# A one-core DiT block: mLSTM products with tokens on partitions, gathered tokens turned once, a smaller first modulation group, and the last dense batch cut in two

## The chip, the cores and the metric

The kernel runs on one core of one Trainium2 chip. The metric is device microseconds of one execution. Times are medians of several runs; the rows below come from one profiled execution of the kernel before.

## The reference

One layer of a diffusion backbone on 256 latent tokens and 256 context tokens of width 2048, in float32. The context is only read by the mLSTM. Cut to what matters here:

```
m_lat, m_ctx = silu(c) @ ada_w + ada_b, silu(c_ctx) @ ada_w + ada_b     # six modulation vectors each
hc = modulate(rmsnorm(x_ctx, norm_mix), m_ctx[0], m_ctx[1])
hl = modulate(rmsnorm(x_lat, norm_mix), m_lat[0], m_lat[1])
pl = hl @ w_in                                                # all heads; hc @ w_in[:, OFF_K:] for the context

# mLSTM, 4 heads x 2 directions, chunks of 128 tokens, one step of the scan:
s   = einsum('bhtd,bhsd->bhts', qc, kc) * exp(log_w - m_t)
num = einsum('bhts,bhsv->bhtv', s, vc) + w_prev * einsum('bhvk,bhtk->bhtv', C, qc)
den = s.sum(-1) + w_prev * einsum('bhk,bhtk->bht', n, qc)
h   = num / maximum(abs(den), exp(-m_t))
# then h_f + h_b, hn = h * rsqrt(mean(h * h, -1) + EPS), sigmoid(o) * hn * g

x_lat = x_lat + m_lat[2] * (y_l @ w_out)                      # y_l: sgu, mLSTM and pooling side by side
hf = modulate(rmsnorm(x_lat, norm_ffn), m_lat[3], m_lat[4])
# PEER: hf @ wq, scores with 2 x 128 keys, top 16 of the 16 x 16 sums: 128 experts per token;
# a = hf . u_tab[e]; w = softmax(scores) * gelu(a); out = sum of w * v_tab[e]
return rmsnorm(x_lat + m_lat[5] * peer_ffn(hf, ...), norm_final)
```

## The kernel before

**Layout and engines.** Activations lie with channels on partitions (xL latent, xC context, 16 tiles of 128 channels by 256 tokens). Weights come in units of 512 KB from HBM on SP's queue (`load`, L273). A unit is copied on ACT to a rounded `hi` part, the rest is formed on DVE as `lo`, and TensorE (PE) multiplies in three passes (hi by hi, hi by lo, lo by hi): 24 matmuls of 256 columns for a unit, tiles named `mm`. One helper records each matmul (L354) and one each DVE and ACT operation (L133), so the tile names tell rows apart. A float32 matmul shows as two records of PE in the trace, one in the listings of the order.

**Order.** All instructions are emitted in one stream per engine by a planner: each stage is a generator that emits a piece and yields an estimated time, and the planner runs beside each other the units of the projections (`step`), the heads (`gen_heads`), the second modulation (`araw`, `adacc`, `adat`), and later the copying of tokens (`copy_hB`). PE has PSUM banks of three tags: `mm` (4 banks), `sm` (3) and one for `ada`.

**The start.** `ada` weights (2 of the 6 modulation vectors) come in 32 ring loads of 1 MB, 5 in flight (RING). Four groups of 512 channels of 8 ring loads each: PE multiplies (`adaps`), ACT copies (`adasb`), PE turns the result onto partitions (`adat`), and DVE forms four operations per 128 channels (`hm`, `xL`, `hm`, `xC`). The first units `wf` (gates and a part of K) are accumulated over the 16 channel tiles, so each of their pieces waits for its group.

**The heads.** For each head and direction `weights` forms sT (source tokens by tokens) and qw; `products` makes num^T (channels on partitions, 128 x 512) by 8 matmuls and den by 7 matmuls of one column; `diagonal` puts 1/den on a diagonal (2 ACT operations) and `spread_out` multiplies it by ones, so that each row holds it (tile `all`). `finish` scales num, and `norm` squares, sums over channels by 8 records of one column (`hss`), again goes through `diagonal` and `spread_out`, and scales.

**PEER.** 64 of the 256 tokens gather their u rows, through one copy of the tokens in rows (`hB`, four tokens' copies of each, half of them at a time); 192 tokens are multiplied densely with the whole u table (`ups`). Then the v rows are gathered: 1 MB per token for the 192 dense tokens, 32 tokens in a batch accumulated in one `y`; `finish(b, y)` turns a batch back, adds the residual, makes the last rmsnorm and stores 256 KB.

Of the kernel before, what the change touches and what calls it, by code (L numbers as in the profile page):

```python
# [32 lines left out]
P = 128  # L33
D = 2048
# [42 lines left out]
LAG = 3.0  # L77
SUB = 8
# [13 lines left out]
AFTER = 1  # L92
PREP = 1
SS_AT = 2
EARLY = 1
LOAD_AT = {2: 1, 3: 1, 4: 1}
FIRST_AT = (3,)
# [81 lines left out]
def build(tc, a, stack, dbg=None):  # L179
# [219 lines left out]

    early = con.tile([P, 1152], F32, name="early", tag="st")  # L400
# [4 lines left out]
    def ada_mm(ps, kp, w):  # L405
        for kk in range(2):
            for part in range(2):
                j = 2 * kk + part
                mm(ps[32 * j:32 * j + 32, :], st[:, 2 * kp + kk, :], w[:, kk, part * 512:part * 512 + 512],
                   start=(kp == 0), stop=(kp == KD // 2 - 1), tile_position=(0, 32 * j))  # L410

    def ada_fin(g, ps, work, tag):

        sb = work.tile([P, 512], F32, name="adasb", tag=tag, bufs=4)
        act.activation(sb, ps, AF.Copy)
        yield 2.0
        pt = sm_ps("adat")
        for q in range(4):
            mm(pt[:, 4 * q:4 * q + 4], sb[:, q * P:(q + 1) * P], sel.rearrange("p a i -> p (a i)"),
               start=True, stop=True)  # L420
        ptv = pt[:, 0:16].rearrange("p (q a i) -> p a i q", a=2, i=2)
        k4 = slice(4 * g, 4 * g + 4)
        for part in range(2):
            b = vecs[:, V_ADAB + part * KD + 4 * g:V_ADAB + part * KD + 4 * g + 4]
            vec.tensor_tensor(mod[:, part, :, k4], ptv[:, part], b[:, None, :].to_broadcast([P, 2, 4]), op=OP.add)
        for i in range(2):
            vec.scalar_tensor_tensor(gm[:, i, k4], mod[:, 1, i, k4], 1.0,
                                     vecs[:, V_NMIX + 4 * g:V_NMIX + 4 * g + 4], op0=OP.add, op1=OP.mult)
        yield 0.0
# [92 lines left out]
    def add_first(src, streams, dones, n_ada, rest):  # L522


        box = {}

        def use(n, q):
            def f(u):
                if q == 0:
# [3 lines left out]
                for kt in range(4):  # L533
# [11 lines left out]

        for q in range(4):
            for n in range(3):
                add(src[n, q], True, use(n, q))
                if q == 3:
                    add_ada(n_ada)  # L550
                    rest(n)
# [31 lines left out]
    def alloc_mixers():  # L583
# [11 lines left out]
        V["Ct"] = b1[:, 4096:8192].rearrange("p (r k v) -> p r k v", r=8, k=2)  # L595
        V["ncol"] = early[:, 1000:1016].rearrange("p (r k) -> p r k", k=2)
        V["kT"] = B.tile([P, 8, T], F32, name="kT")
        V["vlat"] = B.tile([P, 2, 1024], F32, name="vlat")
# [120 lines left out]
    def vm_done(cb):  # L719
        def f(pss):  # L720
            s = slice(cb * 512, cb * 512 + 512)
            for i in range(2):
                act.activation(V["vctx"][:, i, s], pss[2 + i], AF.Copy)
                act.activation(V["vlat"][:, i, s], pss[i], AF.Copy)
# [6 lines left out]
    def gen_C(h, d):  # L731
# [8 lines left out]
        for kt in range(2):  # L740
# [4 lines left out]
            act.activation(V["Ct"][:, r, kt], pc[:, 0:T], AF.Copy)  # L745
            vec.tensor_copy(V["ncol"][:, r, kt:kt + 1], pc[:, T:T + 1])
# [21 lines left out]
    def gen_heads():  # L768
        B, kT, qT, vlat, Ct = V["B"], V["kT"], V["qT"], V["vlat"], V["Ct"]
        rows3, gtok, mask, ncol = V["rows3"], V["gtok"], V["mask"], V["ncol"]  # L770
# [38 lines left out]
        def products(h, d, sT, rng, qw):  # L809
            r, row = d * 4 + h, d * 32 + h  # L810

            blks = (0, 1) if d == 0 else (1, 0)
            pn = mm_ps("num")
            for vt in range(2):
                o = pn[:, vt * T:(vt + 1) * T]
                for n, blk in enumerate(blks):
                    t0, t1 = rng[blk]
                    mm(o[:, t0:t1], vlat[:, blk, h * T + vt * P:h * T + (vt + 1) * P], sT[:, blk, t0:t1],
                       start=(vt == 0 and n == 0), stop=False)
                for kt in range(2):  # L820
                    mm(o, Ct[:, r, kt, vt * P:(vt + 1) * P], qw[:, kt], start=False, stop=(vt == 1 and kt == 1))

            pd = sm_ps("den")
# [10 lines left out]
            return pn, diagonal(den)  # L834

        def diagonal(x):
            dg = B.tile([P, 2, P], F32, name="diag", tag="nB", bufs=1)
            for tb in range(2):
                act.activation(dg[:, tb], ident, AF.Copy, scale=x[:, tb:tb + 1])
            return dg  # L840

        def spread_out(dg):

            pb = sm_ps("all")
            for tb in range(2):
                mm(pb[:, tb * P:(tb + 1) * P], ones, dg[:, tb], start=(tb == 0), stop=(tb == 1))
            return pb[:, 0:T]

        def finish(h, d, pn, dg):
            den = B.tile([P, T], F32, name="E", tag="E", bufs=1)  # L850
            act.activation(den, spread_out(dg), AF.Copy)
            den_b = den[:, None, :].to_broadcast([P, 2, T])
            pnv = pn.rearrange("p (b t) -> p b t", b=2)
            if d == 0:
                hold["hs"] = B.tile([P, 2, T], F32, name="hs", tag="b1")
                vec.tensor_tensor(hold["hs"], pnv, den_b, op=OP.mult)
            else:
                hb = big()
                vec.tensor_tensor(hb, pnv, den_b, op=OP.mult)
                vec.tensor_tensor(hold["hs"], hold["hs"], hb, op=OP.add)  # L860

        def norm(h):
            hs = hold["hs"]
            h2 = B.tile([P, 2, T], F32, name="h2", tag="b2")
            act.activation(h2, hs, AF.Square)
            yield HY4
            pq = sm_ps("hss")
            for tb in range(2):
                for vt in range(2):
                    mm(pq[:, tb:tb + 1], h2[:, vt, tb * P:(tb + 1) * P], ones[:, 0:1],  # L870
                       start=(tb == 0 and vt == 0), stop=(tb == 1 and vt == 1))
            rs = B.tile([P, 2], F32, name="hrs", tag="den", bufs=2)
            rstd_of(rs, pq[:, 0:2], T)
            dg = diagonal(rs)
            yield HY5
            while V.get("o", -1) < 2 * h + 1:
                yield 1.0
            yb = V["yb"][:, 2 * h:2 * h + 2]
            vec.tensor_tensor(hs, hs, spread_out(dg)[:, None, :].to_broadcast([P, 2, T]), op=OP.mult)
            vec.tensor_tensor(yb, yb, hs, op=OP.mult)  # L880

        for h in range(HEADS):
            scores(h)
            yield 2.0
            for d in range(2):
                rest = weights(h, d)
                yield HY1
                pn, dg = products(h, d, *rest)
                yield HY2
                finish(h, d, pn, dg)  # L890
# [199 lines left out]
    hBd = tc.dram_tile([P, D], F32, name="hB_spill")  # L1090

    def copy_hB():

        hf, h64 = R["hf"], R["h64"]
        yield HBY0
        for k0 in range(0, KD, 4):
            k4 = slice(k0, k0 + 4)
            vec.tensor_tensor(h64[:, k4], hf[:, k4, 0, NA:T].bitcast(F32), hf[:, k4, 1, NA:T].bitcast(F32), op=OP.add)
            for g in range(2):
                yield HBY if g == 0 else 1.0  # L1100
                pbt = sm_ps("hbt")
                for k in range(k0, k0 + 4):
                    for r in range(REP):
                        mm(pbt[r * BT:(r + 1) * BT, (k - k0) * P:(k - k0 + 1) * P], h64[:, k, g * BT:(g + 1) * BT],
                           ident, start=True, stop=True, tile_position=(0, r * BT))
# [652 lines left out]
```

## Time and profile before

| what | us |
|---|---|
| median of 3 runs | 1932.53 (1932.23 to 1934.69) |
| profiled execution | 1929.97 |
| its span, first to last instruction | 1928.2 |
| PE busy | 1710.3 (89%) |
| weight loads of PE (beside PE) | 1354.9 (70%) |
| DVE busy | 1226.9 (64%) |
| ACT busy | 701.6 (36%) |
| POOL busy | 382.9 (20%) |

The profiled execution is 2.6 us under the median, and 1.8 us of it lie outside the span. The DMA engines move 670 MB in the span, 348 GB/s in the mean. Busy shares are means over stages with different limits: the table of stretches below tells which engine fills which stage.

### The profile page before, as it was taken

What the parts mean: (1) busy time and instruction counts of PE and PEld (TensorE: products, weight loads), DVE (VectorE), ACT (ScalarE), POOL (GpSimd) and SP (SyncE); (2) the same over time, 40 slices, a digit from 0 to 9 for tenths busy, and PEclk for the clock granted to TensorE, in tenths of its full rate; (3) what the DMA queues carried; (4) which work ended last, traced back from release to release, by engine and by line L of the source; (5) the groups of instructions that cost most, each with busy time, mean ns of one, the idle gap of its engine ahead of it and who ended that gap; (6) DMA issues with size and microseconds to landing.
All of it is one profiled execution on the core that took longest, in us unless ns stands there. A gap on an engine that the chain in (4) does not pass through costs nothing.

```text
span 1928.2 us, 29971 instructions
## 1 busy us (share of the span) xinstructions
PE 1710.3 (89%) x11882; PEld 1354.9 (70%) x11882; DVE 1226.9 (64%) x2498; ACT 701.6 (36%) x1105; POOL 382.9 (20%) x324
## 2 busy tenths in 40 slices
PE   4999999999899899899999899999997777767765
PEld 2689789979899799889888798888873222222221
DVE  5356868776698669989998787777553323323232
ACT  4235335555544444454444454444431101101010
POOL 0000000000000000432333233233223333333331
PEclk8999999999999999999999999999998888888898
DMA  9975878776778754999999999999989999999996
GB/s 395 392 268 186 286 243 294 272 251 221 230 290 329 261 182 151 370 420 417 417 409 419 396 421 421 415 397 392 383 325 409 421 421 421 421 421 421 420 421 276
DMA packets 115870, 670.20 MB, mean 348 GB/s; under 512 B 12689, under 2 KB 15249, under 8 KB 53265
## 3 DMA queue, kind: packets, MB, share of 16 engines
q1 hardware_dynamic: 69648, 332.72, 46.2%
q0 software_dynamic: 46080, 335.56, 42.2%
q8 instruction: 93, 1.52, 0.3%
q14 instruction: 49, 0.39, 0.1%
HBM read 662.99 MB, written 5.24 MB: 347 GB/s over the span
## 4 chain that ended last, share of the span: by engine, by line
PE 69%; DMA 21%; issue 4%; DVE 4%; ACT 1%; POOL 1%; SPq 0%; POOLq 0%; ACTq 0%; DVEq 0%
PE ups L354 29%; PE mm L354 25%; DMA gath<-in_v_rows,iT 6%; DMA raw<-in_v_rows,iT 6%; DMA hB<-in_v_rows,iT 4%; PE adaps L354 3%; PE y L354 2%; PE yb L354 2%; DMA ring<-in_ada 2%; DMA rawB<-in_v_rows,iT 2%; PE num L354 1%; PE sm L354 1%; PE pick L354 1%; DMA rawA<-in_v_rows,iT 1%; DVE lo L133 1%
## 5 line engine op out<-in xcount | busy, mean ns | idle before, releaser
L354 PE MATMUL ups<-hf,hi 128*128 128x384 f32 x2048 | 602.2, 366 | 0.0
L354 PE MATMUL ups<-hf,lo 128*128 128x192 f32 x2048 | 515.0, 251 | 8.2 <-DVE lo L133 8.2
L354 PEld LDWEIGHTS ups<-hf,hi 128*128 128x128 f32 x2048 | 387.0, 189 | 53.7 <-issue 47.8
L354 PEld LDWEIGHTS ups<-hf,lo 128*128 128x128 f32 x2048 | 393.5, 192 | 10.2 <-DVE lo L133 10.1
L133 DVE TENSOR_TENSOR lo<-rawA,hi 128x1024 fp32r<-128x1024 f32 x148 | 180.7, 1222 | 114.2 <-ACT hi L133 107.2
L133 DVE TENSOR_TENSOR lo<-rawB,hi 128x1024 fp32r<-128x1024 f32 x146 | 178.3, 1222 | 105.4 <-ACT hi L133 93.1
L133 DVE SCALAR_TENSOR_TENSOR oh<-c,iT,pick 128x128 f32<-128x128 f32 x192 | 55.3, 344 | 287.0 <-PE pick L354 287.0
L1371 POOL DMA_INDIRECT W<-in_u_rows,iT x34 | 51.5, 1514 | 889.2 <-DMA W<-in_u_t 778.3
L133 ACT ACTIVATE hi<-rawA 128x1024 fp32r<-128x1024 f32 x148 | 156.3, 1056 | 155.8 <-PE ups L354 67.8
L133 ACT ACTIVATE hi<-rawB 128x1024 fp32r<-128x1024 f32 x146 | 154.3, 1057 | 154.4 <-PE ups L354 78.1
L354 PE MATMUL mm<-xL,hi 128*128 128x256 f32 x864 | 181.0, 290 | 4.8 <-ACT xL L133 1.7
L1371 POOL DMA_INDIRECT gath<-in_v_rows,iT x115 | 130.2, 1132 | 251.5 <-PE y L354 128.8
L354 PEld LDWEIGHTS mm<-xL,hi 128*128 128x128 f32 x864 | 144.0, 192 | 14.2 <-issue 7.5
L354 PE MATMUL y<-gath,wA 128*32 128x512 f32 x672 | 106.3, 720 | 52.6 <-DMA gath<-in_v_rows,iT 52.6
L133 DVE SCALAR_TENSOR_TENSOR adacc<-araw,early,adacc 128x1024 f32<-128x1024 f32 x120 | 152.3, 1277 | 0.0
L133 ACT ACTIVATE uA<-uA 128x4 f32<-128x4 f32 x48 | 9.9, 206 | 372.9 <-DVE oh L133 372.9
L354 PE MATMUL mm<-xL,lo 128*128 128x256 f32 x432 | 122.4, 283 | 0.0
L133 ACT ACTIVATE hi<-W 128x1024 fp32r<-128x1024 f32 x76 | 80.5, 1060 | 103.4 <-PE ups L354 98.1
L354 PEld LDWEIGHTS pick<-W,oh 128*128 128x128 f32 x384 | 78.4, 246 | 55.0 <-issue 53.1
L354 PE MATMUL mm<-hf,hi 128*128 128x256 f32 x512 | 98.0, 290 | 6.9 <-ACT hf L133 5.3
L133 DVE TENSOR_TENSOR lo<-W,hi 128x1024 fp32r<-128x1024 f32 x76 | 92.4, 1220 | 16.3 <-ACT hi L133 14.4
L354 PE MATMUL pick<-W,oh 128*128 128x128 f32 x384 | 97.1, 410 | 1.1 <-issue 1.1
(278 smaller groups left out, 2937.3 us busy)
## 6 DMA issues: line engine op xcount, KB each, us to landing
araw<-in_ada SPq DMA_DIRECT2D x128, 512.0 KB, 5.2
W<-in_u_t SPq DMA_DIRECT2D x38, 1024.0 KB, 9.1
rawB<-in_u_t SPq DMA_DIRECT2D x35, 1024.0 KB, 9.6
rawA<-in_u_t SPq DMA_DIRECT2D x35, 1024.0 KB, 9.6
ring<-in_ada SPq DMA_DIRECT2D x32, 1024.0 KB, 12.1
raw<-in_u_t SPq DMA_DIRECT2D x20, 1024.0 KB, 9.5
rawB<-in_wout SPq DMA_DIRECT2D x16, 512.0 KB, 5.6
rawA<-in_wout SPq DMA_DIRECT2D x16, 512.0 KB, 5.5
```

Of the source, the lines that this page charges most:

```text
L133: return f(*args, **kw)
L354: ten.matmul(out, lhsT, rhs, start=start, stop=stop, skip_group_check=True, **kw)
L1371: pool.indirect_dma_start(out=g.raw, out_offset=None, in_=tab, in_offset=bass.IndirectOffsetOnAxis(ap=idx, axis=0))
```

## The change

There are four separate edits.

1. **mLSTM products.** num is made with tokens on partitions: one 128 x 257 tile per block of 128 tokens (two `mm` banks in place of one `mm` and one `sm`). The weights of the matmul are sT and qw, the moving side is v with a column of ones, and the state C with n as its last column, so that column 256 is den. 1/den then stands on the partition of its token, and scaling takes it as a per-partition operand: `diagonal`, `spread_out` and their `all`, `E` and `diag` tiles go. The rmsnorm sums its squares on ACT (accum_out), and four 128 x 128 turns (`hT`) bring the head back to channels on partitions.
2. **Gathered tokens.** `copy_hB` turns 64 tokens once, in 4 groups of 4 matmuls of 64 x 128, in place of 8 groups of 16 matmuls that write 32 partitions each; the spill holds 64 rows, and `load_hB` brings back each half as 4 loads of 32 partitions.
3. **Modulation groups.** Five groups, of 256, 256, 512, 512 and 512 channels, in place of four of 512; for the small ones a ring load holds four channel blocks of 256 columns (8 matmuls). `wf` loads come earlier in SP's queue, and the first units are emitted in halves.
4. **Last batch.** The last 32 dense tokens end in two parts: `finish` runs for 24 tokens while the last 8 are still gathered, and then for 8.

```diff
+LAST = 8
-LOAD_AT = {2: 1, 3: 1, 4: 1}
-FIRST_AT = (3,)
+LOAD_AT = (0, 1)
+FIRST_AT = ((), (1,), (3,), (3,), (3,))
+    GROUPS = ((0, 2), (2, 2), (4, 4), (8, 4), (12, 4))
...
             for tb in range(2):
                 tt = slice(tb * P, (tb + 1) * P)
-                terms = [(sT[:, blk, tt], ones[:, 0:1]) for blk in range(2) if rng[blk][0] <= tb * P < rng[blk][1]]
-                terms += [(qw[:, kt, tt], ncol[:, r, kt:kt + 1]) for kt in range(2)]
+                terms = [(sT[:, blk, tt], vlat[:, blk, h]) for blk in range(2) if rng[blk][0] <= tb * P < rng[blk][1]]
+                terms += [(qw[:, kt, tt], Ct[2 * r + kt]) for kt in range(2)]
+                pn.append(mm_ps("num"))
                 for n, (x, y) in enumerate(terms):
-                    mm(pd[:, tb:tb + 1], x, y, start=(tb == 0 and n == 0), stop=(tb == 1 and n == len(terms) - 1))
+                    mm(pn[tb][:, 0:T + 1], x, y, start=(n == 0), stop=(n == len(terms) - 1))
             den = B.tile([P, 2], F32, name="den", tag="den", bufs=2)
-            act.activation(den, pd[:, 0:2], AF.Abs)
+            for tb in range(2):
+                act.activation(den[:, tb:tb + 1], pn[tb][:, T:T + 1], AF.Abs)
...
+            hs = hold["hs"]
+            for tb in range(2):
+                if d == 0:
+                    vec.tensor_scalar(hs[:, tb], pn[tb][:, 0:T], den[:, tb:tb + 1], None, op0=OP.mult)
+                else:
+                    vec.scalar_tensor_tensor(hs[:, tb], pn[tb][:, 0:T], den[:, tb:tb + 1], hs[:, tb],
+                                             op0=OP.mult, op1=OP.add)
...
+                act.activation(h2[:, tb], hs[:, tb], AF.Square, accum_out=rs[:, tb:tb + 1])
...
+                    ten.transpose(pt[:, vt * T + tb * P:vt * T + (tb + 1) * P], hs[:, tb, vt * P:(vt + 1) * P], ident)
...
+            yield HBY
+            pbt = sm_ps("hbt")
+            for k in range(k0, k0 + 4):
+                mm(pbt[0:NB, (k - k0) * P:(k - k0 + 1) * P], h64[:, k], ident, start=True, stop=True)
+            st_ = R["rs"][1].tile([NB, 512], F32, name="hst", tag="hst", bufs=2)
+            act.activation(st_, pbt[0:NB], AF.Copy)
+            sync.dma_start(hBd[:, k0 * P:(k0 + 4) * P], st_)
+            yield 6.0 - HBY
+        load_hB(0)
...
-            if t % BT == BT - 1:
-                ends.append(finish(t // BT, y))
+            cuts = (BT - LAST, BT) if t >= NA - BT else (BT,)
+            if t % BT + 1 in cuts:
+                t0 = 0 if t % BT + 1 == cuts[0] else cuts[0]
+                ends.append(finish(t // BT, y, t0, t % BT + 1 - t0))
```

On PE, the first products (head 0, direction 0) stood in this order before: num with its two kinds of operands, and then den, with one column of ones or of the state n (in `early`) at a time.

```order
L354 MATMUL num<-sT,vlat 128x256
L354 MATMUL num<-sT,vlat 128x128
L354 MATMUL num<-qw,b_1025 128x256 x2
L354 MATMUL num<-sT,vlat 128x256
L354 MATMUL num<-sT,vlat 128x128
L354 MATMUL num<-qw,b_1025 128x256 x2
L354 MATMUL den<-ones,sT 128x1
L354 MATMUL den<-early,qw 128x1 x2
L354 MATMUL den<-ones,sT 128x1 x2
L354 MATMUL den<-early,qw 128x1 x2
```

In the change the same place holds seven matmuls, and no den.

```order
L353 MATMUL num<-vlat,sT 128x257
L353 MATMUL num<-b_1065,qw 128x257 x2
L353 MATMUL num<-vlat,sT 128x257 x2
L353 MATMUL num<-b_1065,qw 128x257 x2
```

What moved: the first three write the tile of tokens 0 to 127, the other four that of tokens 128 to 255; the two matmuls of `all` that came some 16 rows later are gone.

On DVE, at the end of the last head, this stood before (b_2361 is `yb`, the gated output; `ysplit` is the first operand of the output projection).

```order
L133 RECIPROCAL den<-den 128x2
L133 TENSOR_TENSOR lo_4669<-rawA,hi_4667 128x1024
L133 TENSOR_TENSOR b_2361<-b_2361,mixed 128x256
L133 SCALAR_TENSOR_TENSOR adacc<-araw_4496,early,adacc 128x1024
L133 TENSOR_TENSOR big<-num,E 128x512
L133 TENSOR_TENSOR hs<-hs,big 128x512
L133 TENSOR_SCALAR hrs<-hss 128x2
L133 RECIPROCAL hrs<-hrs 128x2
L133 TENSOR_TENSOR hs<-hs,all 128x512
L133 TENSOR_TENSOR b_2361<-b_2361,hs 128x512
L133 TENSOR_TENSOR ysplit<-b_2361,ysplit 128x256 x16
```

In the change the place reads as follows.

```order
L132 RECIPROCAL den<-den 128x2
L132 TENSOR_TENSOR lo_4569<-rawA,hi_4567 128x1024
L132 TENSOR_TENSOR b_2395<-b_2395,mixed 128x256
L132 SCALAR_TENSOR_TENSOR adacc<-araw_4410,early,adacc 128x1024
L132 SCALAR_TENSOR_TENSOR hs<-num,den,hs 128x256 x2
L132 TENSOR_SCALAR hrs<-hrs 128x2
L132 RECIPROCAL hrs<-hrs 128x2
L132 TENSOR_SCALAR hs<-hs,hrs 128x256 x2
L132 TENSOR_TENSOR b_2395<-b_2395,hT 128x512
L132 TENSOR_TENSOR ysplit<-b_2395,ysplit 128x256 x16
```

What moved: the three operations between the reciprocal and the head (`lo`, `b`, `adacc`) stand ahead of it as before; the scaling takes the reciprocal itself, and the last product reads the turned head from PSUM.

On SP's queue, the start read as follows before (the ring loads are the modulation's, `wf` the first units').

```order
L1467 DMA ring<-in_ada 128x2048 x8
L273 DMA rawA<-in_wf 128x1024
L1467 DMA ring<-in_ada 128x2048
L273 DMA rawA<-in_wf 128x1024
L1467 DMA ring<-in_ada 128x2048
L273 DMA rawB<-in_wf 128x1024
L1467 DMA ring<-in_ada 128x2048 x3
L273 DMA rawB<-in_wf 128x1024
L273 DMA rawA<-in_wf 128x1024 x2
L273 DMA rawB<-in_wf 128x1024
L1467 DMA ring<-in_ada 128x2048 x4
```

In the change it reads:

```order
L1456 DMA ring<-in_ada 128x2048 x3
L272 DMA rawA<-in_wf 128x1024
L1456 DMA ring<-in_ada 128x2048 x3
L272 DMA rawA<-in_wf 128x1024
L1456 DMA ring<-in_ada 128x2048
L272 DMA rawB<-in_wf 128x1024
L1456 DMA ring<-in_ada 128x2048 x2
L272 DMA rawB<-in_wf 128x1024
L272 DMA rawA<-in_wf 128x1024 x2
L272 DMA rawB<-in_wf 128x1024
L1456 DMA ring<-in_ada 128x2048 x8
```

What moved: the first `wf` loads stand behind ring loads 2, 5 and 6 and not behind 7, 8 and 9; ahead of ring load 15, the last of the first 1024 channels, stand seven `wf` loads in both. On PE, 96 matmuls of the first units stand between the beginning and the product with that ring load before, and 120 in the change; 48 before and 24 now stand right behind its `adat`. From the units behind the first three on, PE's order differs only in the heads and the `hbt` pieces, and POOL's not at all.

## Rows read from the trace of the kernel before

**Rows 1.** Stretches: start:end, length, busy (instructions) PE PEld DVE ACT POOL, PEclk, DMA share, GB/s.

```profile
0.00:67.00 67.00, 37.15 (x243) 19.40 (x243) 26.80 (x45) 22.71 (x36) 0.20 (x4) 0.90 0.99 400
...
340.00:520.00 180.00, 178.35 (x1144) 156.92 (x1144) 128.16 (x192) 101.13 (x157) 0.00 (x0) 1.00 0.71 241
...
790.00:1431.00 641.00, 634.93 (x4389) 570.58 (x4390) 507.59 (x764) 299.94 (x438) 198.49 (x130) 0.99 0.99 404
1431.00:1917.00 486.00, 344.68 (x2165) 136.34 (x2168) 156.50 (x722) 38.12 (x84) 174.44 (x186) 0.87 1.00 413
1917.00:1928.20 11.20, 2.15 (x14) 0.92 (x6) 4.23 (x7) 2.74 (x4) 0.00 (x0) 0.73 0.06 23
```

**Rows 2.** Chain of waits, 24 to 80 us: start, us, what ran or was waited for.

```profile
39.86 1.24 DVE hm L133 x3
...
51.88 12.30 DMA ring<-in_ada
...
67.06 5.85 PE sm L354 x48
```

**Rows 3.** Chain of waits, 335 to 390 us (heads).

```profile
346.02 3.04 PE num L354 x16
349.06 1.46 PE den L354 x14
...
353.49 0.44 PE all L354 x4
...
381.36 0.79 PE hss L354 x8
```

**Rows 4.** Chain of waits, 322 to 332 us: products 257 columns wide.

```profile
326.16 1.74 PE pc L354 x8
```

**Rows 5.** Timeline, 397 to 421 us: a scaled head, and PE behind it; waits in brackets.

```profile
397.31 1.03 PE L354 MATMUL num<-qw,b 128*128 128x256 f32 x4
...
404.82 0.68 DVE L133 TENSOR_TENSOR hs<-num,E 128x512 f32<-128x512 f32 x1
...
405.65 0.47 PE L354 MATMUL mm<-hi,xL 128*128 128x512 f32 x1 [0.46 <-DVE hs L133]
```

**Rows 6.** Timeline, 513 to 537 us: the end of the last head.

```profile
516.68 1.03 PE L354 MATMUL num<-qw,b 128*128 128x256 f32 x4
...
519.80 0.70 ACT L133 ACTIVATE diag<-c,den 128x128 f32<-128x128 f32 x2 [0.43 <-DVE den L133]
...
526.52 1.28 ACT L133 ACT_TABLE_LOAD   x1
...
526.55 1.87 PE L354 MATMUL hss<-ones,h 128*128 128x1 f32 x8 [5.41 <-ACT h L133]
...
532.61 0.58 PE L354 MATMUL mm<-ysplit,hi 128*128 128x256 f32 x1 [1.63 <-DVE ysplit L133]
```

**Rows 7.** Chain of waits, 645 to 700 us: the copying of tokens.

```profile
651.62 0.45 PE sc L354 x4
...
657.69 1.01 PE hbt L354 x32
```

**Rows 8.** Timeline, 1916 to 1929 us: the end.

```profile
1918.63 0.66 PE L1592 MATMUL yT<-c,ysb 128*128 128x128 f32 x4 [0.77 <-ACT ysb L133]
1919.32 0.69 DVE L133 TENSOR_TENSOR z<-yT,mod 128x512 f32<-128x512 f32 x1 [17.11 <-PE yT L1592]
...
1920.83 0.63 ACT L133 ACTIVATE sq<-z 128x512 f32<-128x512 f32 x1 [2.26 <-DVE z L133]
...
1921.50 1.01 DVE L133 TENSOR_REDUCE z<-sq 128x32 f32<-128x512 f32 x1 [0.76 <-ACT sq L133]
...
1923.72 0.35 DVE L133 RECIPROCAL z<-z 128x32 f32<-128x32 f32 x1 [0.30 <-ACT z L133]
...
1924.83 0.33 SPq L1611 DMA_DIRECT2D out<-o  x1
```

**Rows 9.** DVE's groups by shape, 1100 to 1115 us: 128 elements per partition.

```profile
L133 DVE TENSOR_TENSOR sc<-sc,W 128x128 f32<-128x128 f32 x1 | 0.3, 292 | 0.0
```

More of the change, by code (lines that the diff above doesn't have):

```diff
@@ L404, in build, with ada_mm @@
     sel = con.tile([P, 2, 2], F32, name="sel")
-    def ada_mm(ps, kp, w):
-        for kk in range(2):
-            for part in range(2):
[L408 to L415, printed above, removed]
+    def ada_mm(ps, nk, kp, w):
+        rows, n = 8 // nk, nk * P
+        w = w.rearrange("p (r a c) -> p r a c", r=rows, a=2)
+        for r in range(rows):
+            k = rows * kp + r
+            for part in range(2):
+                j = 2 * (r % 2) + part
+                mm(ps[32 * j:32 * j + 32, 0:n], st[:, k, :], w[:, r, part], start=(k < 2), stop=(k >= KD - 2),
+                   tile_position=(0, 32 * j))
@@ L532, in f @@
                 lo = u.lo.rearrange("p (j k c) -> p j k c", j=2, c=P)
-                for kt in range(4):
+                for kt in kts:
                     k = 4 * q + kt
@@ L544, in use @@
             return f
+        for n in range(3):
+            add(None, False, use(n, 0, (0, 1)))
         for q in range(4):
             for n in range(3):
-                add(src[n, q], True, use(n, q))
+                u = add(src[n, q], True, use(n, q, (2, 3) if q == 0 else range(4)))
+                if q == 0:
+                    first[n] = u
                 if q == 3:
@@ L810, in products @@
             r, row = d * 4 + h, d * 32 + h
[L812 to L821, printed above, removed]
@@ L833, in products @@
             vec.reciprocal(den, den)
[L834 to L847, printed above, removed]
@@ L864, in norm @@
             h2 = B.tile([P, 2, T], F32, name="h2", tag="b2")
-            act.activation(h2, hs, AF.Square)
+            rs = B.tile([P, 2], F32, name="hrs", tag="den", bufs=2)
+            for tb in range(2):
+                act.activation(h2[:, tb], hs[:, tb], AF.Square, accum_out=rs[:, tb:tb + 1])
             yield HY4
-            pq = sm_ps("hss")
+            rstd_of(rs, rs, T)
             for tb in range(2):
[L869 to L874, printed above, removed]
+                vec.tensor_scalar(hs[:, tb], hs[:, tb], rs[:, tb:tb + 1], None, op0=OP.mult)
             yield HY5
@@ L887, in gen_heads @@
                 yield HY1
-                pn, dg = products(h, d, *rest)
+                pn, den = products(h, d, *rest)
                 yield HY2
-                finish(h, d, pn, dg)
+                finish(h, d, pn, den)
                 yield HY0 if d == 0 else HY3
@@ L1725, in layout @@
         "xc": con(np.concatenate([xT, cT], axis=2)),
-        "ada": con(aw1),
+        "ada": aw1,
         "ada2": con(aw2),
@@ L1756 @@
     out = np.asarray(r.results[0]["out_0"])
-    return np.ascontiguousarray(out.reshape(T // BT, P, KD, BT).transpose(0, 3, 2, 1).reshape(T, D))[None]
+    tokens = []
+    for b in range(T // BT):
+        cut = BT - LAST if b == NA // BT - 1 else BT
+        tokens += [part.reshape(P, KD, -1).transpose(2, 1, 0).reshape(-1, D)
+                   for part in (out[b, :, 0:KD * cut], out[b, :, KD * cut:]) if part.size]
+    return np.ascontiguousarray(np.concatenate(tokens))[None]
```

149 lines of the change are left out of this document (70 added, 79 removed).

## The prediction

> **What bounds the kernel now.** I read the table of stretches first [rows 1], because the busy shares of the whole span mix stages with different limits. Until 67 us the DMA engines are busy 0.99 of the time and PE 37.15 of 67 us: the modulation weights bound the start. From there PE takes over, and in the heads (340 to 520 us) it is busy 178.35 of 180 us, with DVE at 128.16 (71%) and DMA at 0.71. Each microsecond of PE work taken out there moves everything behind it. From 790 to 1431 us PE (634.93 of 641) and DMA (0.99) are both full, from 1431 to 1917 us DMA alone (1.00). I take it that a whole program that comes earlier brings its transfers earlier too, so that a gain ahead of 790 us survives to the end: the bytes that these two stages move are the same and start as much sooner. The last 11.2 us are a serial chain (DMA 0.06, DVE 4.23 us): they count in full.
>
> Then I read the chain of waits at the four edits. At the start [rows 2] PE has run out of work at 51.88 us and waits 12.30 us for a ring load; after its product and turn PE goes through 48 matmuls (5.85 us), and further ones without a wait. In the heads [rows 3] the chain stays on PE, and num, den, `all` and `hss` are links of it.
>
> **Edit 3, modulation groups (−2.5 us).** The load that PE waits for is number 15, with seven `wf` loads ahead of it in both orders, so it lands as before. What changes is how much PE has done by then: 120 matmuls of the first units instead of 96. The 24 more cost 24 x 0.121 = 2.9 us (5.85 / 48 is 0.122) and now lie under the 12.30 us wait. They are gained only if what follows the load can go on as fast: DVE needs four operations of 0.41 us (1.24 / 3) for each 128 channels, 1.65 us, against 12 matmuls of 0.121, 1.45 us, for a half unit; over four tiles PE may lose 4 x 0.2 = 0.8 us. So 2.1 to 2.9, and I take 2.5. Bounds: a loss of 2 us if the earlier `wf` loads (512 KB at the 400 GB/s of [rows 1], 1.3 us each) push a ring load that is wanted sooner; a gain of 5 if the earlier first groups also shorten the wait itself.
>
> **Edit 1, products (−18 us).** num: six 256-wide and two 128-wide matmuls take 3.04 us [rows 3]. The trace holds products of 257 columns, `pc`: 8 records in 1.74 us [rows 4], 0.217 each. Seven matmuls are 14 records, 14 x 0.217 = 3.04 us: no change. They differ from `pc` in that rows of v and C start every 257 elements; should that cost something, it falls on 8 x 14 = 112 records. den goes (1.46 us) and so does `all` (0.44 us) [rows 3]. For seven of the eight pairs of head and direction that is on PE's own path: 7 x 1.90 = 13.3 us. The norms of the first three heads lose `hss` (0.79) and `all` (0.44) and gain four turns of 128 x 128, which take 0.66 us in the tail with the first one's start [rows 8] and about 0.55 in a full queue: 3 x 0.68 = 2.0 us.
>
> The last pair and the last norm lie in the drain, where PE waits. num ends at 517.71 us (516.68 + 1.03), and PE goes on with the output projection at 532.61 [rows 6]: 14.9 us. In the new order DVE still has `lo`, `b` and `adacc` between the reciprocal and the head, but ACT loses the diagonal (0.70 us [rows 6]) and den's 1.46 us, so `hi`, `lo` and the rest come about 2.2 us earlier; two scalings of 256 columns, 0.42 us each (between 0.29 for 128 columns [rows 9] and 0.69 for 512 [rows 8]), replace two of 0.69: another 0.5. Behind it, Square with a sum, in two halves, costs 0.5 us more than in one; the table load of 1.28 us, which now lies beside `hss` (526.52 and 526.55, [rows 6]), stands alone, but `hss` itself (1.87 us [rows 6]) is gone: −0.6 net; then no diagonal, no `all`, but the turn and two scalings: about −0.9. Together −2.2 − 0.5 + 0.5 − 0.6 − 0.9 = −3.7, and I take −4 (bounds −2 and −6). The trace has the table load at 1.28 us [rows 6]. The Trainium skill, page "ScalarE: Activation LUTs", section "What ACT_TABLE_LOAD costs", adds to a load of about 1283 ns a drain of some 1380 ns, 2.66 us for each switch; the load agrees with the row, the drain no row here shows apart. By that figure the drain term would be some 1.4 us smaller, an estimate from that page.
>
> 13.3 + 2.0 + 4 = 19.3 us. Against it stand new waits: each pair now holds two of the four `mm` banks, and they come free with the scaling on DVE. Before, one bank was held from num's end at 398.3 us to 405.50, 7.2 us, and one matmul of PE waited 0.46 us for it [rows 5]. In the new order two units' first matmuls of the same stage wait for such a bank. I take 1.3 us for all of it: −18. Bounds: −21 (drain −6) and −12 (a wait of 0.9 us in each of eight pairs).
>
> **Edit 2, gathered tokens (−4.6 us).** Eight pieces `hbt` of 1.01 us lie on PE's chain [rows 7]: 8.1 us. The new groups have 4 matmuls, 8 records, of 128 moving columns; the nearest row, `sc`, has 4 such records in 0.45 us [rows 7], so a group takes 0.88 and four 3.5 us: −4.6 (bounds −3 and −5). Before, a record cost 1.01 / 32 = 0.032 us, now 0.11: the small ones were cheap. That is what a rule says that speaks against this edit: the Trainium skill, "TensorE: Matmul & The Clock Gate", section "Part 3: Packing small matmuls — row/col tiling", has tiles of the array working side by side when the matmuls are given a tile position. The rows agree; counting matmuls alone (256 records to 32) would give −7.1, the rows −4.6. The spill and the loads of `hB` add a wait on SP's queue, behind which the next weight loads stand; DMA is not full here, and the units are some microseconds ahead, so I cost it at nothing, and at 1.5 us if that cover is gone (in the bound −3).
>
> **Edit 4, the last batch (−2.5 us).** The last chain now works on 128 columns instead of 512. Operations of 128 elements take 0.29 us [rows 9]; those of the end take 0.69 and the sum 1.01 [rows 8]. Three products on the path: 3 x 0.40 = 1.2; the sum 0.7; Square, 0.63 on ACT, by about half, 0.3; the reciprocal, 0.35, by about 0.2: 2.4. The copy from PSUM and the turn stay. The store issued at 1924.83 carries 64 KB instead of 256; the span ends 3.4 us after it: 0.1 more (0 to 0.5). The 24 tokens' chain has 8 tokens' gathers, 8 x 2.6 = 21 us, as its cover (POOL's 186 instructions, its gathers, in 486 us [rows 1], are 2.6 us each). −2.5, bounds −1.5 and −3.
>
> **Sum.** −2.5 − 18 − 4.6 − 2.5 = −27.6. On the profiled execution, 1929.97 us, that is 1902.4; this execution lies 2.6 us under the median of 1932.53, so 1905 on that basis. The bounds of the terms, all at one end, are −34 (1898) and −14.5 (1918).
>
> **Rivals.** (a) The products' gain turns into waits: DVE, at 71% in the heads, gets the scalings in more pieces, and PE waits for banks or for sT. 1.5 us of waits for each of eight pairs take 12 us: 1917; with the start's 2.5 lost as well 1919.5. For it: the 7.2 us between num and the scaling [rows 5]. Against: the planner's stages stand apart, and only 0.46 us was waited.
>
> (b) More is gained: the drain loses 10 of its 14.9 us instead of 4, because ACT and DVE are no longer behind, and the start gains 5 instead of 2.5: 1905 − 8.5 = 1896.5. For it: that PE waits there for a chain of small operations, of which several go; against: the three of DVE that stand ahead of the scaling stay.
>
> (c) The change does not reach the end: if the stage from 1431 us, at DMA 1.00 [rows 1], were held by something that does not start earlier, only edit 4 would remain: 1930, no difference. Against: its first gathers are released by PE's work on the dense table.
>
> (d) Slower: PE runs into a lack of `mm` banks at every product. With two banks held by num and one by the unit before, the next unit but one must wait until DVE scales; the place is the heads, the price up to 7.2 us [rows 5] for each of eight pairs. It decides from 31.5 / 8 = 3.9 us for each, where it eats the 27.6 and the 0.2% on top. At 5 us a pair: 1932.5 + 40 − 27.6 = 1945. Against: 7.2 us are 2.5 units of 2.9 us, each with one bank, and there are two left; and only two first matmuls in PE's new order wait so.
>
> **How the numbers follow.** I give the forecast (1898 to 1917) 0.70, (a), which reaches from there to 1922, 0.14, (b) 0.06, (c) 0.05, (d) 0.05. The predicted time is 1905. A range from 1896 to 1921 leaves (c), (d) and the edges of (a) and (b) out. A change of under 0.2% (3.9 us) is what this measurement could not tell from none. Faster by more: 0.70 + 0.14 + 0.06 = 0.90; within: (c), 0.05; slower: (d), 0.05.
>
> **What the new profile would show.** No den, `all` or `hss` on PE; num 3.0 us a pair and, in the heads, a PE as full as before; the output projection's first matmul some 10.9 us after the last num, and about 24 us earlier in the span than 532.61; `hbt` 0.88 us four times; the last sum on DVE at about 0.3 us; the wait for ring load 15 some 3 us shorter and its end unmoved. The forecast is wrong if PE has new idle times that DVE's `hs` ends, if num takes clearly over 3.1 us, if the first `ups` does not come earlier by what the heads gained, or if the gathers' stage grows by what came before.

## The result, and the profile after

The change takes 1910.05 us (median of 4 runs, 1908.01 to 1912.84) against 1932.41 before (4 runs): ratio 0.9883, 95% interval 0.9869 to 0.9897, 22.4 us less. The forecast was 1905 (27.5 less), its range 1896 to 1921. The profiled execution takes 1911.3 us, its span 1909.5, 18.7 less than the span before; it is one of the slower of the four.

The table of stretches of the change, cut at about the same work as in [rows 1] (columns as there):

```profile
0.00:67.00 67.00, 39.27 (x323) 23.88 (x323) 27.39 (x49) 21.89 (x37) 0.20 (x4) 0.92 0.99 402
...
340.00:500.00 160.00, 157.09 (x951) 134.95 (x950) 123.74 (x194) 93.09 (x145) 0.00 (x0) 1.00 0.79 265
...
770.00:1411.00 641.00, 631.50 (x4361) 566.46 (x4361) 504.48 (x762) 299.14 (x437) 195.00 (x126) 0.99 0.99 400
1411.00:1898.00 487.00, 347.76 (x2188) 141.43 (x2191) 161.74 (x731) 41.09 (x89) 175.66 (x187) 0.87 1.01 415
1898.00:1909.50 11.50, 4.79 (x22) 1.41 (x14) 1.83 (x7) 1.11 (x3) 0.00 (x0) 0.50 0.02 8
```

The stages look as before: PE fills the heads, PE and DMA both the dense table, DMA the v rows. Where the time went is seen by following one piece of work from stage to stage, before and after. The first ups and the first yb by their tiles (records, ns least/median/most, first and last start), before:

```profile
L354 PE MATMUL ups<-hf,hi x2048: 355/362/669, 750.0 to 1432.6; 128*128 128x384 f32 x187
...
L354 PE MATMUL yb<-W,wB x104: 592/605/617, 1141.1 to 1355.3; 128*32 128x512 f32 x104
```

and in the change:

```profile
L353 PE MATMUL ups<-hf,hi x2048: 355/362/667, 726.9 to 1416.3; 128*128 128x384 f32 x187
...
L353 PE MATMUL yb<-W,wB x104: 592/605/617, 1124.7 to 1338.9; 128*32 128x512 f32 x104
```

At the first ups the change is 23.1 us ahead (726.9 for 750.0), at the first yb only 16.4 (1124.7 for 1141.1): the stage in which this table of experts is multiplied gave back 6.7 us. (Such places come from the one profiled execution of each kernel.) The same reading at the other places: the last `pc` product starts 1.6 us *later* (329.1 for 327.5), the last num 13.9 us earlier (503.4 for 517.3), the output projection's first pass behind the heads 17.8 us earlier, the first ups 23.1, the first yb 16.4, and the span ends 18.7 us earlier. So per edit, in the two profiled executions:

| stretch | forecast | measured |
|---|---|---|
| start to the last `pc` (modulation groups) | −2.5 | +1.6 |
| last `pc` to last num (products, three norms) | −14 | −15.5 |
| last num to the output projection (drain) | −4 | −3.9 |
| first to last `sc` (turning 64 tokens) | −4.6 | −4.9 |
| first ups to first yb (not in the sum) | 0 | +6.7 |
| last chain | −2.5 | −1.6 |

The measured terms add up to −17.6; the other 1.1 us lie in small pieces between these places.

The 6.7 us were lost in two parts. Timeline of the change, 748 to 780 us:

```profile
768.99 0.53 PE L353 MATMUL ups<-hf,lo 128*128 128x192 f32 x1 [5.66 <-DVE lo L132]
```

and of the kernel before, 771 to 801 us:

```profile
790.55 0.53 PE L354 MATMUL ups<-hf,lo 128*128 128x192 f32 x1 [4.07 <-DVE lo L133]
```

At this wait, some 40 us into the stage, 1.6 us were lost; from it to the first yb the change takes 355.7 us and the kernel before 350.6, 5.1 us more.

**The start.** Chain of waits of the change, 24 to 80 us:

```profile
53.33 10.95 DMA ring<-in_ada
...
64.33 1.98 PE adaps L353 x8
...
66.97 1.87 PE adat L353 x8
68.84 5.26 PE sm L353 x24
```

The same pieces took 1.11 us (adaps x8), 1.05 (adat) and 2.9 (24 of the 48 of [rows 2]) before: PE ran at the lower of its two clock levels from 64.3 to 74 us (granted clock 0.59 in the mean from 64 to 76 us; 1.00 before), and these pieces grew by 4.0 us together. What this cost further on is read below.

**The heads.** Chain of waits, 325 to 390 us, to be set beside [rows 3]:

```profile
347.56 3.04 PE num L353 x14
350.60 7.19 PE mm L353 x60
...
363.35 3.04 PE num L353 x14
...
382.69 0.81 PE hT L867 x4
```

num takes 3.04 us with 14 records of 257 columns, as worked out, and the next row is plain projection work: den and `all` are gone. The turn `hT` took 0.81 us here and 0.72 and 0.55 in the two heads after it. From the start of the last `pc` to that of the last num PE is idle for 2.91 us (busy 171.39 of 174.30), against 1.65 before (188.15 of 189.80).

**The drain.** Timeline, 502 to 517 us, beside [rows 6]:

```profile
503.19 0.60 PE L353 MATMUL num<-Ct,qw 128*128 128x257 f32 x2
...
508.94 0.87 DVE L132 SCALAR_TENSOR_TENSOR hs<-num,den,hs 128x256 f32<-128x256 f32 x2
...
510.37 1.28 ACT L132 ACT_TABLE_LOAD   x1
...
512.51 1.16 PE L867 MATMUL hT<-c,hs 128*128 128x128 f32 x4 [7.31 <-DVE hs L132]
...
514.79 0.58 PE L353 MATMUL mm<-ysplit,hi 128*128 128x256 f32 x1 [0.90 <-DVE ysplit L132]
```

From num's end (503.79) to the projection's product it is 11.0 us, against 14.9; 10.9 was forecast. The table load stands alone now, 1.28 us; the next activation begins 0.02 us behind it (511.67), and from the load's end to the product it takes 3.1 us against 4.8 before.

**The tokens and the end.** A `hbt` group took 1.02 us, four times, where 0.88 was worked out. Timeline of the end, beside [rows 8]:

```profile
1899.66 1.93 PE L353 MATMUL y<-gath,wA 128*32 128x512 f32 x8 [0.52 <-DMA gath<-in_v_rows,iT]
...
1902.37 1.12 PE L1582 MATMUL yT<-c,ysb 128*128 128x128 f32 x4 [0.78 <-ACT ysb L132]
...
1904.58 0.38 DVE L132 TENSOR_REDUCE z<-sq 128x8 f32<-128x128 f32 x1 [0.43 <-ACT sq L132]
...
1906.64 0.33 SPq L1601 DMA_DIRECT2D out<-o  x1
```

The sum fell from 1.01 to 0.38 us, the store is issued 2.9 us before the end of the span (3.4 before), but the last product took 1.93 us and the turn 1.12 (0.66 before): here too PE was at its lower clock (granted clock 0.50 in the stretch); before, the last product took 1.06 us.

### The profile page after: what moved, and what is told of

It is laid out like the page before. It is cut to its first block, busy times and chain, and to the rows that moved or that the text cites. A ratio compares the mean times of both kernels' runs of the same rounds, so it can differ in the third digit from the quotient of the medians.

```text
span 1909.5 us, 29276 instructions
## 1 busy us (share of the span) xinstructions
PE 1691.9 (89%) x11536; PEld 1338.4 (70%) x11536; DVE 1224.6 (64%) x2502; ACT 691.7 (36%) x1093; POOL 380.3 (20%) x324
## 4 chain that ended last, share of the span: by engine, by line
PE 69%; DMA 22%; DVE 5%; issue 3%; ACT 1%; POOL 0%; SPq 0%; POOLq 0%; DVEq 0%; ACTq 0%
PE ups L353 30%; PE mm L353 25%; DMA gath<-in_v_rows,iT 7%; DMA hB<-in_v_rows,iT 5%; PE y L353 3%; PE adaps L353 3%; DMA raw<-in_v_rows,iT 2%; PE yb L353 2%; DMA rawB<-in_v_rows,iT 2%; DMA ring<-in_ada 2%; DMA rawA<-in_v_rows,iT 2%; PE sm L353 1%; PE pick L353 1%; DVE lo L132 1%; PE num L353 1%
## 5 line engine op out<-in xcount | busy, mean ns | idle before, releaser
L132 ACT ACTIVATE hi<-W 128x1024 fp32r<-128x1024 f32 x76 | 80.4, 1060 | 104.7 <-PE ups L353 97.2
```

Source lines behind the costliest of these rows:

```text
L132: return f(*args, **kw)
```

## The experiments

All were run beside the kernel before, in three groups of four; the kernels of a group share the runs of the kernel before (medians 1930.99, 1933.5 and 1932.23 us), so across groups ratios are compared and not times.

**Modulation groups undone** (`no_groups`), groups, loads and first units of before:

```diff
-    GROUPS = ((0, 2), (2, 2), (4, 4), (8, 4), (12, 4))
...
-    for g, (k0, nk) in enumerate(GROUPS):
+    for g in range(4):
```

> The change with the modulation groups of before (four of 512 channels, wf loads and first units as before). Theory: in the profiled run of the change the smaller groups moved 24 matmuls under the loads (-2.9 us), but TensorE then ran at the lower granted clock from 64.3 to 74 us (adaps 1.98 for 1.11, adat 1.87 for 1.05, sm x24 5.26 for 2.92: +4.0 us), so undoing them gives the change's 1910 us or 1 to 2 us less, with pc starting at 236 us as before. Rival (the prediction's term, the clock only an accident of one run): undoing them costs 2.5 us, 1912.5, and pc starts later than in most executions of the change.

1911.48 us, ratio 0.9897 (0.988 to 0.9913): the interval overlaps the change's, and the total does not settle it. The profile does: pc began at 239.4 us, the latest of all so far, because PE's clock fell there as well (0.60 from 64 to 68, 0.55 to 72 us). The fall is thus no product of the small groups. That part of the theory fell, and the clock must be held equal before the groups can be judged.

**Gaps filled** (`clock_kept`):

```diff
+            if n in (14, 15):
+                dum = sm_ps("dum")
+                for _ in range(6):
+                    ten.matmul(dum[:, 0:P], ident, ident, start=True, stop=True, skip_group_check=True)
             ada_mm(ps, nk, kp, ring[n])
```

> The change, with six 128 x 128 matmuls on the identity, which nothing reads, ahead of the products with ring loads 14 and 15, so that TensorE's idle time there (1.42 us twice) is filled. Theory (clock): granted clock 1.0 from 64 to 74 us, sm x24 2.9 us, about 4 us less than a run of the change in which it fell: 1907 to 1908 in all runs, and a smaller spread than 1908.0 to 1912.8. Rival: the clock in that stretch does not hang on these gaps, and the time is the change's 1910 us with the same spread.

1909.32 us (1904.88 to 1910.22), ratio 0.9877 (0.9858 to 0.9896): not clear of the change, and the spread is no smaller. In its profile the granted clock was 1.00 from 42 us to the first pc, as intended, and pc began at 235.9 us: 1.7 earlier than in the change's profile, and only 0.3 earlier than before (236.2). By this pair of profiles the lower clock cost 1.7 us at the first pc, not the 4 us by which the pieces grew, and the groups themselves gained 0.3 and not 2.5.

**One load of 128 partitions** (`hb_one_load`):

```diff
+            for r in range(REP):
+                sync.dma_start(hBr[r * BT:(r + 1) * BT, k0 * P:(k0 + 4) * P], st_[BT:NB])
...
-                load_hB(1)
+                sync.dma_start(R["hB"], hBr)
```

> The change, with the second half's rows spilled four times (128 rows) and brought back by one load of 128 partitions in place of four loads of 32 partitions. Theory: in the change the four loads hold the DMA engines at 250 GB/s for some 18 us (1042 to 1060 us of the profiled run, share 1.0), the u table's next rows land late and TensorE loses 5.5 us there; with one load the rate stays above 400 GB/s and the time falls by 5 to 6 us, to 1904.5, with the second half's yb at most 22 us after... that is, 21.5 us earlier than before and not 16.4. Rival: it is chance of the transfers' order in one run; the time stays at 1910 us.

1904.72 us (1904.24 to 1908.7), ratio 0.9865 (0.9848 to 0.9882); first ups to first yb 390.7 us, as before (391.1), against 397.8 in the change. The interval overlaps the change's (0.9869 to 0.9897), so this stretch of the profile decides and not the total: from the wait for `lo` (4.99 us here) to the first yb it takes 349.2 us, against 355.7. The rate of the DMA engines shows why. Rates (GB/s in 40 equal slices) of the change, 1020 to 1080 us, with the engines' busy share in tenths above:

```profile
DMA  9998999999999999999999999999999999999999
GB/s 426 421 404 360 399 410 431 426 426 404 431 426 426 399 431 333 279 208 246 257 268 251 251 257 350 404 437 415 410 421 426 410 437 415 421 426 410 393 284 415
```

of the kernel before, the same work, 1041 to 1101 us:

```profile
GB/s 410 421 404 388 415 431 437 399 421 431 415 421 431 415 421 431 415 421 437 388 426 415 426 415 431 421 421 421 426 415 431 393 399 339 431 235 295 421 431 295
```

and with one load, 1020 to 1080 us:

```profile
GB/s 426 431 399 415 399 431 431 421 415 399 426 431 355 388 410 426 426 415 415 426 421 415 426 426 415 431 410 421 415 426 415 426 366 388 350 235 415 426 421 251
```

In the change the rate lies between 208 and 279 GB/s for 12 us behind the four loads' issue at 1037 to 1039 us, with the engines busy all the time; then the u table's rows come late, and PE, which has no slack in this stage, waits. Timeline of the change, 1050 to 1068 us:

```profile
1062.98 1.06 ACT L132 ACTIVATE hi<-rawA 128x1024 fp32r<-128x1024 f32 x1 [9.17 <-DMA rawA<-in_u_t]
...
1064.52 1.06 PE L353 MATMUL adaps<-W,wB 128*32 128x512 f32 x8 [2.50 <-ACT wB L132]
```

ACT waits 9.17 us for a load of the u table, `wB` stands behind that on ACT, and PE waits 2.50 us for `wB`; with one load and in the kernel before PE has no wait at this place.

**Last batch in one** (`one_batch`):

```diff
-LAST = 8
+LAST = 0
```

> The change, with the last 32 dense tokens finished in one part (LAST = 0). By the prediction 2.5 us slower than the change, 1912.5; by the profiled run of the change, whose last y ended at 1901.6 us and whose span ended 7.9 us later against 10.4 us before (1917.8 to 1928.2), also 2.5, of which the lower clock in the tail takes some. Rival: the split saves only what the DVE operations show, and loses it to the products of the last 8 tokens waiting for the copy of y: within 1 us of the change.

1914.09 us (1912.14 to 1914.24), ratio 0.9904 (0.9887 to 0.992), slower than the change by 2.1 thousandths, some 4 us, with intervals that overlap; by the prediction's term it would be 2.5 us. From the start of the last token's product to the end it took 11.5 us, against 9.8 in the change. It also shows what the earlier 24 matmuls run into where the clock holds. Its chain of waits, 60 to 110 us:

```profile
66.55 1.07 PE adat L353 x8
...
71.72 5.94 PE mm L353 x45
...
80.44 9.86 DMA ring<-in_ada
...
93.17 7.35 PE sm L353 x48
```

The chain hangs on a ring load from 80.4 to 90.3 us, but that is again the load's time under way and not PE's idle time. PE's own waits stand in its timeline, 66 to 96 us:

```profile
71.72 0.39 PE L353 MATMUL mm<-xC,hi 128*128 128x256 f32 x1 [0.41 <-DVE xC L132]
...
90.33 1.06 PE L353 MATMUL adaps<-ring,early 128*32 128x512 f32 x8 [0.44 <-DMA ring<-in_ada]
```

PE catches up with DVE's modulated tiles (the four matmuls from 70.4 us on take 1.5 us, where four take 0.5 at their usual pace, so about 1.0 us is lost) and then waits 0.44 us for the ring load; the kernel before has neither wait. Its chain stayed on PE from 64.2 us on and reached the same `adat` at 92.48, here 92.12. (The 7.35 us of sm, 5.85 at full clock, are another fall: granted clock 0.63 from 92 to 96 us.)

**The change again** (`control`):

> The change as it is, beside the next three on the same chip. 1908 to 1912 us by its first runs; the stretch from the first ups to the first yb 397 to 399 us (391 before), if the reload of hB costs 6 us in every run and not in one.

1910.85 us, ratio 0.9882 (0.9863 to 0.9901): the first result holds; first ups to first yb 396.8 us, 354.7 of them behind the wait for `lo`.

**Turning of before** (`no_turn`):

```diff
+                    for r in range(REP):
+                        mm(pbt[r * BT:(r + 1) * BT, (k - k0) * P:(k - k0 + 1) * P], h64[:, k, g * BT:(g + 1) * BT],
+                           ident, start=True, stop=True, tile_position=(0, r * BT))
```

> The change with copy_hB of before (8 groups of 16 small matmuls; the second half spilled in 128 rows and brought back by one load). Theory: the turn's gain (first to last sc 98.5 us before, 93.6 in the change: 4.8 us) comes back and the reload's loss (first ups to first yb 391 and 398 us: 6.5) goes, so 1.5 to 2 us faster than the control. Rival (the prediction's term alone): 4.6 us slower than the control.

1909.47 us (1907.78 to 1909.9), ratio 0.9875: 1.4 us under the control, within the intervals, and surely not 4.6 above it. First to last sc 98.5 us (93.7 in the control), first ups to first yb 390.9, 350.2 of them behind the wait for `lo`: gain and loss as the theory has them.

**Four loads from rows of their own** (`hb_four_from_128`) and **one load of repeated rows** (`hb_repeat`):

```diff
 # hb_four_from_128: spill of hb_one_load
+                for r in range(REP):
+                    sync.dma_start(R["hB"][r * BT:(r + 1) * BT], hBr[r * BT:(r + 1) * BT])
 # hb_repeat: spill of the change
+                sync.dma_start(R["hB"], hBd[BT:NB][None].to_broadcast([REP, BT, D]))
```

> The change with the second half spilled in 128 rows, as in the kernel with one load, but brought back by four loads of 32 partitions, each from rows of its own. If the 32 partitions of a load are what slows the transfers: the rate falls to about 250 GB/s for some 18 us as in the change, first ups to first yb about 397 us, time as the control. If it is that the same 32 rows are read four times: 391 us, and 5 to 6 us faster than the control.

> The change with one load of 128 partitions in place of the four, which reads the same 32 rows of the 64-row spill four times. If the 32 partitions are the cause: 391 us from the first ups to the first yb, and 5 to 6 us faster than the control (1904.5). If the repeated rows are: as the control.

Four loads from distinct rows: 1909.89 us, ratio 0.9879, first ups to first yb 397.3, 355.2 of them behind the wait for `lo`: as the control. So it is the four loads into 32 partitions each, and not the rows that they read. Over all profiles but that with repeated rows, this part takes 354.7 to 357.4 us in the six kernels with four loads and 349.0 to 351.5 in the seven with one: the reload costs some 5.4 us. The wait for `lo` itself, some 270 us ahead of the reload, lies between 4.3 and 5.7 us with four loads and between 4.1 and 5.0 with one; what sets it is open. The Trainium skill, "SBUF — State Buffer", section "Door 1: The DMA port swizzle (why `[64,N]` ≈ `[32,N]`)", has 32 consecutive partitions reach 8 of 16 ports, half of the rate; the 208 to 279 GB/s beside 420 fit that, other transfers being under way beside the load. Four transfers of 256 KB in place of one of 1 MB, into all partitions each, were not run: that it is the partitions and not the number of transfers is not shown apart.

The repeated rows went as neither theory expected: 1927.27 us, ratio 0.9975 (0.9965 to 0.9985), 16 us slower than the control, 412.3 us from first ups to first yb. PE waits 17.6 us for one operation. DMA share and rate of this kernel, 1060 to 1085 us:

```profile
DMA  9999889989999999765422222222222210093799
GB/s 262 236 328 275 197 236 328 262 223 301 288 249 275 275 275 262 249 275 210 170 118 118 105 105 105 105 105 105 105 105 105 92 66 39 26 170 66 288 419 433
```

At its end only a quarter of the engines work, at a quarter of the rate (105 of 420 GB/s). The Trainium skill, "DMA: Bandwidth & Descriptors", section "Why a DMA increments its semaphore by 16 and not by 1", has the number of engines of a transfer divide the slowest dimension of both sides; here that is 4 (the repeats), which agrees. As a test of the rows this kernel is worthless, since it changed the number of engines too; the one load from 128 rows and the four loads from them are the pair that decides.

**Products alone** (`products_only`), the kernel before with the first edit:

```diff
-            pd = sm_ps("den")
...
+                pn.append(mm_ps("num"))
```

> The kernel before with the new products, scaling and norm alone (old groups, old turning of tokens, last batch in one). By the traces: last pc to last num 189.8 us before and 174.3 in the change (-15.5), last num to the output projection's second pass 15.7 and 11.8 us (-3.9): 19.4 us faster than before, ratio 0.990. The prediction said 18. Rival (half of it eaten by waits for mm banks): 9 us, ratio 0.995.

1912.77 us against 1932.23, ratio 0.9902 (0.9887 to 0.9918): 19.5 us. The waits for banks that would have taken half of it are not there: PE's idle time from the last `pc` to the last num is 2.9 us, against 1.65 before.

**One load and filled gaps** (`one_load_clock`), with the two edits shown above:

> The change with one load of 128 partitions for the second half's rows and with the twelve filling matmuls ahead of the products with ring loads 14 and 15. Theory: the reload's 6 us and the lower clock at the start come off: first ups to first yb 391 us, pc from 236 us, 27 to 28 us faster than before, ratio 0.9857. Rival (the clock falls elsewhere instead): 25 us, as with the one load alone.

1902.64 us (1901.96 to 1903.43), ratio 0.9848 (0.9834 to 0.9861): faster than both kernels, 29.6 us under the one before, where 27 to 28 were expected. First ups to first yb 389.9 us; pc from 236.8.

**The same with the groups of before** (`one_load_clock_old_groups`), the edit of `no_groups` on it:

> The same kernel with the modulation groups of before, the filling matmuls in the same place. Theory: at the full clock the smaller groups gain nothing, since TensorE, 24 matmuls ahead, waits for ring load 23 instead: pc from 236.2 us (235.9 with the small groups), the same time within 1 us. Rival (the prediction's term): 2.5 us slower than with the small groups.

1906.99 us (1902.38 to 1908.59), ratio 0.9862 (0.9846 to 0.9879). The time is not the same within 1 us, as the theory had it: the totals speak for the small groups, by 4 us with intervals that overlap, and pc begins at 240.7 us. The profile shows the clock again. Up to 94 us the two kernels are level (sm from 93.99 and from 94.13 us). Then, chain of waits of this kernel, 93 to 140 us:

```profile
93.99 5.85 PE sm L355 x48
...
122.19 8.29 PE sm L355 x48
```

the same piece takes 5.85 us at 94 and 8.29 at 122 us, at a granted clock of 0.67, behind a wait of 0.92 us for a ring load that no matmul fills. Its fastest run, 1902.38, is level with the other kernel's median.

All the profiles together help to separate the clock from the groups. The first pc starts as follows (us).

| granted clock at the start | groups of before | small groups |
|---|---|---|
| 1.00 from 60 to 140 us | 236.2, 236.5 | 235.9, 235.9, 236.1, 236.8 |
| falls at 64 us | 239.4 | 236.9, 237.2, 237.6, 237.6 |
| falls at 92 us | none | 237.3, 238.7 |
| falls at 120 us | 240.7 | none |

At the full clock the small groups gain nothing that can be told; where the clock falls at 64 us, pc begins about 2 us earlier with them, though one profile stands on the other side.

**The end filled too** (`one_load_clock_tail`):

```diff
+            if t >= NA - LAST:
+                dum = mm_ps("dum")
+                for _ in range(4):
+                    ten.matmul(dum[:, 0:P], ident, ident, start=True, stop=True, skip_group_check=True)
             add_rows(y, w[:, i], got.popleft(), t % BT == 0, t % BT == BT - 1)
```

> The kernel with one load and filled gaps, with four more 128 x 128 matmuls that nothing reads ahead of each of the last 8 dense tokens' products. Theory: the lower clock that the change's profile shows in the tail (y 1.94 for 1.06, yT 1.12 for 0.66) costs 1.3 us there, and goes: last y to the end of the span 7.6 us instead of 9.0. Rival: the filling matmuls themselves delay the products, or the clock does not follow them: no gain or 1 us slower.

1902.45 us, ratio 0.9848: no gain that can be told. Timeline, 1875 to 1902 us:

```profile
1892.37 1.07 PE L353 MATMUL y<-gath,wA 128*32 128x512 f32 x8 [0.43 <-DMA gath<-in_v_rows,iT]
1894.21 0.66 PE L1590 MATMUL yT<-c,ysb 128*128 128x128 f32 x4 [0.78 <-ACT ysb L132]
```

The clock holds (1.07 and 0.66 us): from the start of the last token's product to the end it takes 8.3 us against 9.6 without, and the filling did not delay it (it starts 774.1 us behind the first yb, 774.0 without). The 1.3 us are thus there in the profile. That the total does not show them fits the rest of this execution, in which first ups to first yb, a stretch that the edit does not touch, took 392.5 us for 389.9, and the totals of this kernel spread from 1901.10 to 1904.75 us.

## Why the prediction was right, and where its terms were off

The time lay in the range and the sign was right; the gain was 22.4 us of 27.5 forecast.

- **Products** (−18): right, and with its mechanism. −15.5 in the heads, −3.9 in the drain, 19.5 us when made alone. The 1.3 us taken off for new waits came about: PE's idle time in the heads rose by 1.26 us (1.65 to 2.91). DVE's `hs` does end new waits of PE there, the first sign of being wrong that the prediction names, but small ones: 1.42 us once, against 0.46, and 0.4 and 0.7 us ahead of two turns. PE's busy time there fell by 16.8 us (188.15 to 171.39), where the sum took 15.3 out; in which rows the other 1.5 us lie is open. The drain's total was met in part by luck: the scaling began 1.6 us earlier behind num, for 2.2, and the part behind it became shorter by 1.8 us, for 1.0. Rivals (a) and (d) fell.
- **Tokens** (−4.6): the piece on PE was right (−4.9). The step that failed is "I cost it at nothing, and at 1.5 us if that cover is gone": I looked at the spill's wait on SP's queue in a stage where DMA had room, and not at the second half's reload, which falls into the stage from 790 us with DMA at 0.99 [rows 1]. Same bytes, but into 32 partitions at a time: some 5.4 us. The gain and the loss of the edit about cancel; without it the total is 1.4 us lower, within the intervals. A `hbt` group took 1.02 us for 0.88: a size.
- **Modulation groups** (−2.5): the step that failed is "PE has run out of work at 51.88 us and waits 12.30 us for a ring load". That row of [rows 2] is the life of a transfer; PE was busy in most of it, as its timeline before, 46 to 70 us, shows:

```profile
61.74 1.06 PE L354 MATMUL adaps<-ring,early 128*32 128x512 f32 x8 [1.25 <-DMA ring<-in_ada]
...
64.23 1.07 PE L354 MATMUL adaps<-ring,early 128*32 128x512 f32 x8 [1.43 <-DMA ring<-in_ada]
```

In the change the same two waits are 1.42 us each, and the row is 1.35 us shorter and not 3. PE was ahead by the 24 matmuls, but what follows could not go on as fast: in the profiles with the clock at 1.00 up to there, PE lost about 1.0 us to DVE's tiles, near the 0.8 that the prediction allowed for, and 0.4 to 1.4 us to the next group's last ring load, which it did not look at. At the full clock the groups are worth nothing that can be told. They do seem to make a fall of the clock cheaper (the table of pc above): where it falls at 64 us, pc begins about 1 us later with the small groups and 3 us later with those of before. The two totals that lean to the small groups (`no_groups` and the last pair, each with intervals that overlap) may come from this, and then by another mechanism than the forecast's; that is not shown.
- **Last batch** (−2.5): −1.6 by the profile, an estimated −2.9 at the same clock (0.87 us of y and 0.46 of yT were the clock's). A size, not a step.
- **To the end** (rival (c)): fell. What was not lost ahead of the first yb came through the DMA-bound stage: 16.4 us ahead at the first yb, 16.8 at the last y. The output projection's first product came 17.8 us earlier and not "about 24": the terms that lie ahead of it in the sum make 20.5, since the tokens come behind it.

## What to carry to other kernels

A transfer in the chain of waits tells how long it was under way, not how long an engine stood still: read the waiting engine's own gaps before booking a gain against it, and ask which load it waits for next. A transfer that is cut up by partitions is to be priced in the stage where it runs: where DMA is full, the same bytes in four loads, each into a quarter of the partitions, cost some 5.4 us more. And effects of one or two microseconds are read from places in the trace at equal clock, since the totals of one kernel here spread by 4 to 5 us.

## What was not expected of the hardware

- Four loads of 256 KB into 32 partitions each held all DMA engines busy at 208 to 279 GB/s in place of 420, for 12 us.
- One load of 1 MB whose source repeats 32 rows four times ended at 105 GB/s with a quarter of the engines busy, and cost 16 us.
- PE's granted clock fell to its lower level between 60 and 140 us in some executions and not in others of nearly the same order: at 64 us (the change, `control`, `hb_one_load`, `hb_repeat`, `no_groups`), at 92 (`one_batch`, `no_turn`), at 120 (`one_load_clock_old_groups`), each time behind waits of 0.4 to 1.4 us for ring loads; not at all before and in `products_only` and `hb_four_from_128`, which have such waits too. With twelve matmuls that nothing reads it stayed up at 64 us in all four profiles that had them; without them it did so in five of ten.
